# Sums of x in two SwiGLU heads tied behind the low parts of weights, and TensorE kept in the order in which the program is written

## The chip, the cores and the metric

The kernel runs on one core of one Trainium2 chip. The metric is the device time of one execution in microseconds; lower is better. The chip's records name five engines: PE (TensorE, the matmuls), PEld (its weight loads), DVE (VectorE), ACT (ScalarE), POOL (GpSimd) and SP (SyncE, which here only issues transfers).

## The reference, cut to what matters

A decoder trunk of two layers on 512 tokens of width 1024: a recurrent mixer, a SwiGLU, dilated attention with shared keys and values, and a second SwiGLU. The change touches the two SwiGLU stages alone:

```python
def swiglu(h, w_in, w_out):                 # w_in: 1024 x 5632, w_out: 2816 x 1024
    g, u = jnp.split(h @ w_in, 2, axis=-1)
    return (jax.nn.silu(g) * u) @ w_out
# in the trunk, for both layers
h = h + swiglu(rms_norm(h, ffn_norm), w_in, w_out)
```

## The kernel before, in words

**Two parts of each number.** Every matmul is done in a rounded format, so each operand is split into a high part (ScalarE rounds it: names that end in h, wh for weights) and a low part (VectorE subtracts the high part: names that end in l, wl). `mm3` issues three matmuls for each term: high by high, low by high, high by low. A weight piece is 128 x 1024; it becomes usable when ScalarE has made wh and VectorE wl.

**The first product of a SwiGLU.** The hidden width 2816 is 22 blocks of 128. Blocks 0 and 1 (two gate blocks, two up blocks) are plain: 24 matmuls of 128x512 each (`plain_block`), and `plain_pair` then forms silu(g) times u. From block 2 on, two gate and two up blocks make a pair q (1 to 10), and its product is worked out from seven products of half size instead of eight, as in Winograd's form of Strassen's scheme. The weights are the gate halves GA and GB, the up half UB, and sums of halves S1 to S4; S1 and S3 are made by transfers that add to what a first transfer has brought (the first issued by SP, the adding one by POOL), and VectorE makes S2 = S1 + GA and S4 = GB + S2 in place. The other factors are quarters of x (B11, B21, B22: four feature blocks by 256 tokens) and sums of quarters T1 to T4, which are made once for each SwiGLU, at its start: `make_t1` to `make_t4`, from the stream h with VectorE (differences, combinations, low parts) and ScalarE (gains, high parts). In the order, `gh<-h` and `gl<-gh,par` are such steps; T4 is written into a free quarter of xh and xl. Each of the seven products is 24 matmuls of 128x256.

**Accumulators.** GA.B11, S2.T2, S3.T3 and UB.T4 add up in one PSUM bank, S1.T1 and S4.B22 in a second, GB.B21 stands in a third. What the bank holds in between is needed too: after GA, after S2 and after S3 ScalarE copies the shared bank to SBUF (`COPY e<-ps`, L690), and after S3 VectorE adds to that copy what is in S1's bank (`e<-ps,e`, L692). So S2.T2 may not begin before the copy after GA, S3.T3 not before the copy after S2, UB.T4 not before the copy after S3, and S4.B22 not before the addition at L692. `gate` (L668 to L670) finishes half a gate block, `store` splits the finished pair for the second product (L277, L278).

**The second product** takes four hidden blocks at a time, as soon as they are stored: an out block ("O" in the table `PRODUCTS`) is two outputs of 12 matmuls of 128x512 each. The last six hidden blocks, which hold the last pair (ghx, glx), are multiplied after all pairs, in eight blocks of 18 matmuls (`p.last`).

**What sets the order.** The program is written as a list of steps (`p.steps`). A scheduler of the Tile layer places the instructions of all engines from it and may move instructions of one engine past each other where no data forbids it; what is written under `tc.high_priority()` is preferred. Each engine then works through its own queue in the order fixed at build time. `Stream` makes the splits of a weight piece one or two pieces ahead. The pool "wts" has three buffers for wh and wl, so the split of a piece waits until the piece three before it has been multiplied.

## Time and profile before

| | |
|---|---|
| median of 3 runs (lowest, highest) | 1196.01 us (1193.79, 1197.9) |
| the profiled execution's own time | 1193.76 us |
| its span, first to last instruction | 1191.5 us |
| PE busy | 1172.9 us, 98% |
| DVE busy | 862.8 us, 72% |
| ACT busy | 621.3 us, 52% |
| DMA, mean over the span | 142 GB/s |

Times inside the execution are given from the start of the span. The first SwiGLU starts near 152 us and its seven-product pairs at 176 us; they end at 471 us. The second one's pairs run from 861 us to 1155 us. "Busy" of PE is of modelled matmul ends, so that a matmul's duration is longer than the distance from its start to that of the next; the distance is what counts for PE's pace, and the same holds for the short overlap of DVE's and ACT's instructions.

### The profile page before, as it was taken

Reading aid. Unit: us, or ns where it says so; the run is one execution under the profiler, and the core shown is the slowest. Engines: PE = TensorE matmul, PEld = TensorE weight load, DVE = VectorE, ACT = ScalarE, POOL = GpSimd, SP = SyncE. Lnnn points to the kernel's source line nnn. Section 1 sums busy time; section 2 is a strip of 40 time slices with the busy share of each in tenths; the row PEclk is TensorE's granted clock in tenths of the full one; section 3 lists DMA queues with packets and bytes.
Section 4 is the critical chain, followed back from the end, with each engine's and each line's share of the span. In section 5 each row is a group of like instructions: output and inputs, shape, how many; then the busy total and the mean of one; then the engine's idle time right before and its main releaser. Section 6 shows DMA issues by size and latency. Waiting matters only on the chain.

```text
span 1191.5 us, 18092 instructions
## 1 busy us (share of the span) xinstructions
PE 1172.9 (98%) x7083; PEld 1040.8 (87%) x7083; DVE 862.8 (72%) x1505; ACT 621.3 (52%) x877; POOL 165.7 (14%) x181
## 2 busy tenths in 40 slices
PE   9999999999999999999999999999999999999998
PEld 6788888999999998888888888898899999999986
DVE  7987679777777776977565677765897777777763
ACT  6796545443444443565555667655563444444431
POOL 4210010000000000020411334341100000000000
PEclk9999999999999999999999999999999999999999
DMA  7643375565555542333988657535855555555413
GB/s 234 153 110 106 106 220 154 157 159 159 144 148 153 157 102 73 111 99 92 226 179 181 143 118 175 106 72 124 230 154 148 159 158 150 151 152 153 101 54 110
DMA packets 71574, 169.30 MB, mean 142 GB/s; under 512 B 6081, under 2 KB 6977, under 8 KB 71489
## 3 DMA queue, kind: packets, MB, share of 16 engines
q1 hardware_dynamic: 52752, 122.36, 32.4%
q0 software_dynamic: 17584, 44.57, 21.9%
q10 hardware_dynamic: 1152, 1.23, 0.3%
q8 instruction: 55, 0.90, 0.3%
q14 instruction: 31, 0.25, 0.1%
HBM read 164.99 MB, written 2.10 MB: 140 GB/s over the span
## 4 chain that ended last, share of the span: by engine, by line
PE 91%; DVE 4%; ACT 2%; DMA 1%; issue 1%; ACTq 0%; DVEq 0%
PE ps L156 25%; PE ps L157 25%; PE ps L158 25%; PE ps L949 5%; PE ps L950 5%; PE ps L951 5%; PE ps L1028 1%; DMA S<-in_f_in 1%; PE ps L1115 1%; DVE xc L444 1%; ACT wh L110 0%; ACT pr L1101 0%; DMA wr<-in_w_in 0%; PE ps L294 0%; DVE ql L278 0%
## 5 line engine op out<-in xcount | busy, mean ns | idle before, releaser
L156 PE MATMUL ps<-xh,wh 128*128 128x256 f32 (+1 forms) x896 | 283.5, 317 | 2.4 <-ACT xh L272 1.4
L158 PE MATMUL ps<-xh,wl 128*128 128x256 f32 (+1 forms) x896 | 281.3, 314 | 2.2 <-DVE wl L615 2.2
L157 PE MATMUL ps<-xl,wh 128*128 128x256 f32 (+1 forms) x896 | 281.3, 314 | 0.1
L110 ACT CAST wh<-wr 128x1024 fp32r<-128x1024 f32 (+2 forms) x132 | 130.8, 992 | 112.0 <-PE ps L157 73.7
L156 PEld LDWEIGHTS ps<-xh,wh 128*128 128x128 f32 x896 | 170.9, 191 | 16.7 <-ACT xh L272 2.3
L158 PEld LDWEIGHTS ps<-xh,wl 128*128 128x128 f32 x896 | 171.0, 191 | 12.4 <-DVE wl L615 2.4
L157 PEld LDWEIGHTS ps<-xl,wh 128*128 128x128 f32 x896 | 171.0, 191 | 10.8 <-DVE xl L278 0.4
L117 DVE TENSOR_TENSOR wl<-wr,wh 128x1024 fp32r<-128x1024 f32 (+3 forms) x89 | 100.1, 1126 | 40.7 <-ACT wh L110 40.2
L602 POOL DMA_DIRECT2D S<-in_f_in x40 | 47.8, 1194 | 583.4 <-DVE w L698 156.2
L156 PE MATMUL ps<-gh,wh 128*128 128x512 f32 x320 | 125.1, 391 | 1.7 <-ACT wh L110 1.7
L157 PE MATMUL ps<-gl,wh 128*128 128x512 f32 x320 | 125.0, 391 | 0.0
L158 PE MATMUL ps<-gh,wl 128*128 128x512 f32 x320 | 124.7, 390 | 0.0
L614 ACT CAST wh<-S 128x1024 fp32r<-128x1024 f32 x60 | 63.0, 1050 | 114.0 <-PE ps L157 69.7
L949 PE MATMUL ps<-wh,xh 128*128 128x512 f32 x224 | 91.5, 408 | 0.0
L951 PE MATMUL ps<-wh,xl 128*128 128x512 f32 x224 | 87.7, 391 | 0.0
L950 PE MATMUL ps<-wl,xh 128*128 128x512 f32 x224 | 87.4, 390 | 0.0
L614 ACT CAST wh<-GB 128x1024 fp32r<-128x1024 f32 x40 | 42.0, 1050 | 83.9 <-PE ps L157 78.2
L615 DVE TENSOR_TENSOR wl<-S,wh 128x1024 fp32r<-128x1024 f32 x60 | 73.3, 1222 | 16.6 <-ACT wh L614 16.6
L714 DVE TENSOR_TENSOR h<-h,ps 128x512 f32<-128x512 f32 x64 | 43.9, 685 | 45.0 <-PE ps L158 45.0
L156 PEld LDWEIGHTS ps<-gh,wh 128*128 128x128 f32 x320 | 60.2, 188 | 13.7 <-ACT wh L110 2.1
L158 PEld LDWEIGHTS ps<-gh,wl 128*128 128x128 f32 x320 | 60.1, 188 | 12.1
L157 PEld LDWEIGHTS ps<-gl,wh 128*128 128x128 f32 x320 | 60.2, 188 | 11.5
(286 smaller groups left out, 2689.9 us busy)
## 6 DMA issues: line engine op xcount, KB each, us to landing
S<-in_f_in SPq DMA_DIRECT2D x40, 512.0 KB, 3.6
S<-in_f_in POOLq DMA_DIRECT2D x40, 512.0 KB, 7.1
wr<-in_f_out SPq DMA_DIRECT2D x32, 512.0 KB, 4.2
wr<-in_w_q SPq DMA_DIRECT2D x28, 512.0 KB, 6.7
wl<-in_w_q POOLq DMA_DIRECT2D x28, 512.0 KB, 7.4
GA<-in_f_in SPq DMA_DIRECT2D x20, 512.0 KB, 3.7
GB<-in_f_in SPq DMA_DIRECT2D x20, 512.0 KB, 6.3
UB<-in_f_in SPq DMA_DIRECT2D x20, 512.0 KB, 5.0
```

Of the source, the lines that this page charges most:

```text
L110: nc.scalar.copy(hi[:, c], r[:, c])
L117: a = eng.tensor_tensor(lo[:, c], r[:, c], hi[:, c].bitcast(F32), ALU.subtract)
L156: PE.matmul(ps, wh, xh, start=first, stop=False, skip_group_check=on)
L157: PE.matmul(ps, wh, xl, start=False, stop=False, skip_group_check=on)
L158: PE.matmul(ps, wl, xh, start=False, stop=last, skip_group_check=on)
L602: nc.gpsimd.dma_start(r, p.half(1, q, n == "S1"), accum_op=ALU.add)
L614: S.copy(hi, r)
L615: V.tensor_tensor(lo, r, hi.bitcast(F32), ALU.subtract)
L714: V.tensor_tensor(h[m + b], h[m + b], ps, ALU.subtract)
L949: PE.matmul(ps[t], xh[k][:, r], wh[:, c], start=k == 0, stop=False)
L950: PE.matmul(ps[t], xh[k][:, r], wl[:, c], start=False, stop=False)
L951: PE.matmul(ps[t], xl[k][:, r], wh[:, c], start=False, stop=k == 7)
```

## The change: what it does

It has four parts.

1. **PE in program order.** The loop over `p.steps` and over `p.last` stands under `tc.manual_schedule` for PE: its instructions stand as they are written, while the other engines are still placed by the scheduler.
2. **Sums of x and plain pairs, held.** `Held` wraps VectorE and ScalarE. While a mark is set, every instruction issued through the wrapper is tied behind that mark in its own engine's order (`behind` makes an order and no wait). The marks are the low parts of the weight pieces of pair 1: `plain_pair(0)` goes behind the low part of S1, `make_t3` behind that of S2, `plain_pair(1)` behind that of GB, `make_t4` behind that of S3. `make_t1` and `make_t2` are not held. The table `early` places them after later steps than before. Held instructions show the line of the wrapper, L70, in the changed program.
3. **Another place for one out block**: in the last pair, the out block stands behind S3.T3 instead of GB.B21 (`LAST_PRODUCTS`).
4. **Banks**: the first plain block takes bank X, the other three take mm banks, instead of the rotation.

```diff
+LAST_PRODUCTS = ["S1.T1", "S2.T2", "GB.B21", "S3.T3", "O", "S4.B22", "UB.T4"]
 PRODUCTS = ["S1.T1", "S2.T2", "GB.B21", "O", "S3.T3", "GA.B11", "S4.B22", "O", "UB.T4"]
...
+class Held:
+    def __init__(self, tc, engine):
+        self.tc, self.engine, self.mark = tc, engine, None
+    def __getattr__(self, op):
+        fn, mark = getattr(self.engine, op), self.mark
+        def run(*a, **k):
+            inst = fn(*a, **k)
+            behind(self.tc, inst, mark)
+            return inst
+        return run if mark is not None else fn
...
-    V, S, G, PE = nc.vector, nc.scalar, nc.gpsimd, nc.tensor
+    V, S, G, PE = Held(tc, nc.vector), Held(tc, nc.scalar), nc.gpsimd, nc.tensor
+    def hold(mark, *fns):
+        V.mark = S.mark = mark
+        for fn in fns:
+            fn()
+        V.mark = S.mark = None
...
-                for name in PRODUCTS:
+                for name in PRODUCTS if q + 1 < HB // 2 else LAST_PRODUCTS:
...
-                    V.tensor_tensor(lo, r, hi.bitcast(F32), ALU.subtract)
+                    p.marks[q, n] = V.tensor_tensor(lo, r, hi.bitcast(F32), ALU.subtract)
...
-                ps = bank()
+                ps = bank("mm" if plain else "X")
...
-                if b == 1:
-                    plain["w"] = pair_tile()
-                    plain_pair(0)
-                elif b == HB + 1:
-                    plain_pair(1)
-                    store(0, plain["w"])
...
-            early = {0: [make_t1], 1: [make_t2], 2: [make_t3], 3: [make_t4]}
-            for s, (kind, *what) in enumerate(p.steps):
-                {"plain": plain_block, "product": product, "out": out_block}[kind](*what)
-                run(early.get(s, ()))
+            first = N_PLAIN
+            early = {0: [make_t1], 2: [make_t2],
+                     3: [lambda: hold(p.marks[first, "S1"], lambda: plain_pair(0))],
+                     5: [lambda: hold(p.marks[first, "S2"], make_t3)],
+                     6: [lambda: hold(p.marks[first, "GB"], lambda: plain_pair(1))],
+                     7: [lambda: hold(p.marks[first, "S3"], make_t4)]}
+            with tc.manual_schedule(engines={mybir.EngineType.PE}):
+                for s, (kind, *what) in enumerate(p.steps):
+                    {"plain": plain_block, "product": product, "out": out_block}[kind](*what)
+                    run(early.get(s, ()))
+                for m, i in enumerate(p.last):
...
```

In the quoted orders lines are those of each program's own file: the low part of a weight piece of the first product is L615 before and L639 after, the addition after S3 is L692 before and L714 after, and L70 is the wrapper.

**VectorE at the first SwiGLU's first pair.** Before, between the low part of GB for this pair and the addition after S3 (`e<-ps,e`, L692; S is the raw tile of S1 or S3 by its number):

```order
L615 TENSOR_TENSOR wl_1639<-GB,wh_1638 128x1024
L278 TENSOR_TENSOR gl<-w,gh 128x1024
L612 TENSOR_TENSOR GB<-GB,S_1383 128x1024
L615 TENSOR_TENSOR wl_1673<-S_1388,wh_1672 128x1024
L278 TENSOR_TENSOR xl<-gl,xh 128x4x256
L615 TENSOR_TENSOR wl_1705<-GA,wh_1704 128x1024
L668 TENSOR_TENSOR e<-ps,e 128x512
L669 TENSOR_TENSOR e<-e,rb 128x512
L615 TENSOR_TENSOR wl_1737<-GB,wh_1736 128x1024
L615 TENSOR_TENSOR wl_1769<-UB,wh_1768 128x1024
L692 TENSOR_TENSOR e<-ps,e 128x512
```

The sums of x are done by then; T4's low part (`xl<-gl,xh`) was the last of them, six rows ahead of the addition. Now, the last rows up to the same addition (L714) and T4's low part:

```order
L639 TENSOR_TENSOR wl_1739<-GB,wh_1738 128x1024
L70 TENSOR_TENSOR w<-w,g 128x512
L691 TENSOR_TENSOR e<-e,rb 128x512
L70 SCALAR_TENSOR_TENSOR gl<-gh,par 128x256 x2
L639 TENSOR_TENSOR wl_1771<-UB,wh_1770 128x1024
L70 TENSOR_TENSOR gl<-w,gh 128x1024
L70 SCALAR_TENSOR_TENSOR gl<-gh,par 128x256
L639 TENSOR_TENSOR wl_1802<-S_1642,wh_1801 128x1024
L70 SCALAR_TENSOR_TENSOR gl<-gh,par 128x256
L633 TENSOR_TENSOR S_1642<-S_1642,GA 128x1024
L714 TENSOR_TENSOR e<-ps,e 128x512
L70 TENSOR_TENSOR xl<-gl,xh 128x4x256
```

Moved: held steps (L70) and the next pair's S1 and S2 (S_1642) now stand ahead of the addition, and T4's low part behind it. The queue of the second SwiGLU reads the same.

**TensorE inside a later pair**, from the end of GA.B11 for the next pair to S4.B22. Before (xh, xl with 128x256 are the quarters B11 and B22; gh with 128x512 is the out block's first matmul):

```order
L157 MATMUL ps<-xl,wh_1972 128x256
L158 MATMUL ps<-xh,wl_1973 128x256
L156 MATMUL ps<-gh,wh_2036 128x512
L156 MATMUL ps<-xh,wh_2004 128x256
L157 MATMUL ps<-xl,wh_2004 128x256
```

Now:

```order
L180 MATMUL ps<-xl,wh_1974 128x256
L181 MATMUL ps<-xh,wl_1975 128x256
L179 MATMUL ps<-xh,wh_2006 128x256
L180 MATMUL ps<-xl,wh_2006 128x256
L181 MATMUL ps<-xh,wl_2007 128x256
```

The one matmul of the out block that stood between the two products is back at its block, behind S4.B22.

**TensorE where the last pair is first used** (ghx; glx is its low part). Before, the matmuls ahead of the first ghx are of the third of the last eight blocks (wh_4479), those of the first two blocks (wh_4407, wh_4442) standing before them:

```order
L158 MATMUL ps<-gh,wl_4443 128x512
L156 MATMUL ps<-gh,wh_4479 128x512
L157 MATMUL ps<-gl,wh_4479 128x512
L158 MATMUL ps<-gh,wl_4480 128x512
L156 MATMUL ps<-ghx,wh_4407 128x512
L156 MATMUL ps<-ghx,wh_4442 128x512
L156 MATMUL ps<-gh,wh_4479 128x512
```

Now, the first block alone:

```order
L179 MATMUL ps<-gh,wh_4409 128x512
L180 MATMUL ps<-gl,wh_4409 128x512
L181 MATMUL ps<-gh,wl_4410 128x512
L179 MATMUL ps<-ghx,wh_4409 128x512
L180 MATMUL ps<-glx,wh_4409 128x512
L181 MATMUL ps<-ghx,wl_4410 128x512
```

Before the first ghx stand 27 matmuls of the three blocks, partly ahead of the last pair's products; now the 12 of the first block, all behind UB.T4.

## The prediction

> **What bounds the kernel now.** I read the page first: where the span goes by engine, and which engine the chain of work that ended last runs through.

> ```profile
> span 1191.5 us, 18092 instructions
> PE 1172.9 (98%) x7083; PEld 1040.8 (87%) x7083; DVE 862.8 (72%) x1505; ACT 621.3 (52%) x877; POOL 165.7 (14%) x181
> ```

> PE is the bound, so only two things can move the time: PE's waits, and its pace. The change removes and adds no matmul. I therefore took PE's timeline in the two SwiGLU stages, where the instructions move, for its pace and its waits. Columns: start, duration, instruction, in brackets the idle time before it and its releaser.

> ```profile
> 176.05 0.28 PE L156 MATMUL ps<-xh,wh 128*128 128x256 f32 x1
> 176.16 0.28 PE L157 MATMUL ps<-xl,wh 128*128 128x256 f32 x1
> ...
> 184.97 0.38 PE L158 MATMUL ps<-xh,wl 128*128 128x256 f32 x1 [2.21 <-DVE wl L615]
> ...
> 196.41 0.59 PE L156 MATMUL ps<-xh,wh 128*128 128x256 f32 x2
> ```

> ```profile
> 867.83 0.38 PE L156 MATMUL ps<-T2h,wh 128*128 128x256 f32 x1 [1.02 <-ACT e L690]
> ...
> 880.02 0.39 PE L156 MATMUL ps<-xh,wh 128*128 128x256 f32 x1 [0.42 <-ACT e L690]
> 880.74 0.38 PE L156 MATMUL ps<-xh,wh 128*128 128x256 f32 x1 [0.34 <-DVE e L692]
> ```

> The seven-product pairs begin with GA.B11 at 176.05. A matmul of 128x256 follows the last one after 0.12 us, so a product of 24 lasts 2.88. The first head waits 2.21 us for the low part of a weight; the second has three shorter waits, together 1.8. The two rows of 880 and the one of 196.41 (two matmuls, one of UB.T4 and then S4.B22's first, at about 196.6) are the places where S4.B22 starts: after GA, S1, S2, GB, S3 and the next GA, in both kernels. They are my yardstick: whatever moved before them, the same six products and one more matmul (0.12 us) have been done.

> **The change part by part.**

> *The heads.* S4.B22 adds to the bank of S1.T1, so it waits until VectorE has read that bank for the sum after S3 (L692). VectorE works off its queue one by one, so I ask when it reaches that addition now. Its chain starts with the low part of S1, which no reordering can bring forward: the raw S1 comes by two transfers, and the cast waits for the second.

> ```profile
> 174.00 1.05 ACT L614 CAST wh<-S 128x1024 fp32r<-128x1024 f32 x1 [4.37 <-DMA S<-in_f_in]
> ```

> ```profile
> 858.78 1.05 ACT L614 CAST wh<-S 128x1024 fp32r<-128x1024 f32 x1 [4.62 <-DMA S<-in_f_in]
> ```

> VectorE's own rows, the start of the chain in each head, and a stretch of six that gives the step of every kind:

> ```profile
> 175.08 1.23 DVE L615 TENSOR_TENSOR wl<-S,wh 128x1024 fp32r<-128x1024 f32 x1 [3.54 <-ACT wh L614]
> ...
> 178.83 0.42 DVE L560 TENSOR_TENSOR gh<-h 128x256 f32<-128x256 f32 x1
> 179.17 0.68 DVE L659 TENSOR_TENSOR g<-ps,rb 128x512 f32<-128x512 f32 x1
> 179.77 0.68 DVE L661 SCALAR_TENSOR_TENSOR w<-ps,rb 128x512 f32<-128x512 f32 x1
> 180.37 0.47 DVE L568 SCALAR_TENSOR_TENSOR gl<-gh,par 128x256 f32<-128x256 f32 x1
> 180.77 1.23 DVE L615 TENSOR_TENSOR wl<-S,wh 128x1024 fp32r<-128x1024 f32 x1
> 181.91 0.68 DVE L662 TENSOR_TENSOR w<-w,g 128x512 f32<-128x512 f32 x1
> ```

> ```profile
> 859.86 1.22 DVE L615 TENSOR_TENSOR wl<-S,wh 128x1024 fp32r<-128x1024 f32 x1 [3.61 <-ACT wh L614]
> ```

> From start to start: 1.14 us for 1024 elements, 0.60 for 512, 0.40 for a combination of 256, 0.34 for a difference of 256. The changed queue has, from S1's low part up to the addition: 13 of 1024 (low parts of S1, S2, GB, S3, the next GA, S4, UB, the next S1; the sums S2, S4 and the next S2; T3's low part; the plain pair's store), 8 of 512 (six of the plain pairs and two of the gate), 8 combinations and 4 differences (T3 and T4). That is 13 x 1.14 + 8 x 0.60 + 8 x 0.40 + 4 x 0.34 = 24.2 us, and the addition itself 0.68. S4.B22 starts at 175.08 + 24.9 = 200.0 in the first head, at 859.86 + 24.9 = 884.8 in the second. Against about 196.6 and 880.74, with the one matmul added, that is 3.5 and 4.2 us late. Before, a part of this work stood ahead of S1's low part, in the 3.5 us in which VectorE waited for it, or ahead of that wait; the hold puts it behind.

> What else waits in the heads lies inside this. S2's and GB's low parts now come in time (at 180.4 and 183.5, needed at about 182 and 184.9), so the 2.21 us go. S3.T3 waits for the copy after S2, which stands on ScalarE behind two gains that wait for the last differences of T3; with the 18th row of the chain, 12.8 us after 175.08, these are done, the gains and the copy take one more:

> ```profile
> 166.79 0.90 ACT L564 ACTIVATE gh<-gh,par 128x256 f32<-128x256 f32 x2
> ```

> ```profile
> 184.76 0.58 ACT L690 COPY e<-ps 128x512 f32<-128x512 f32 x1
> ```

> With half of 0.90 and 0.58 the copy ends at 189.0; without waits S3.T3 would start at 176.05 + 4 x 2.88 = 187.6. So PE waits 1.4 us there, then does S3 and the next GA until 194.8, and waits 5.2 us for the addition. T4's low part follows the addition by 1.2 us and is covered by S4.B22's 2.88. The POOL and SP queues read as before, so transfers come as before. Sum of the heads: +7.7 us, from below 2 (if VectorE does 3 us of each chain in gaps that I count as full) to 9.

> *Inside later pairs.* Before, S4.B22 would come slightly too early for the same addition, and one out matmul fills the gap.

> ```profile
> 252.82 0.68 DVE L692 TENSOR_TENSOR e<-ps,e 128x512 f32<-128x512 f32 x1
> ```

> ```profile
> 253.23 0.28 PE L158 MATMUL ps<-xh,wl 128*128 128x256 f32 x1
> 253.35 0.39 PE L156 MATMUL ps<-gh,wh 128*128 128x512 f32 x1
> 253.58 0.36 PE L156 MATMUL ps<-xh,wh 128*128 128x256 f32 x1
> 253.78 0.28 PE L157 MATMUL ps<-xl,wh 128*128 128x256 f32 x1
> ```

> ```profile
> 222.37:253.51 31.14, 31.14 (x217) 29.14 (x216) 22.69 (x24) 13.12 (x16) 2.39 (x2) 1.00 0.57 153
> ```

> The addition ends at 253.50, GA's last product slot at 253.35. Without the filler S4.B22 waits about 0.2 us, and a first matmul after a wait takes 0.08 more than its step (253.58 to 253.78). A pair is 7 x 2.88 + 48 x 0.227 = 31.05 us of matmuls plus 0.2 to 0.28; before it is 31.14 (the row above, one pair). So +0.1 to +0.2 in each of 8 pairs of both stages: +2.2 us, from 0 to 4.5 (0.28 in 16 pairs, nothing given back).

> *The last pair and its out block.* Before, the out block stands after GB and PE waits 0.85 us for its weights, 1.0 from start to start; the tail is covered.

> ```profile
> 463.05 0.28 PE L158 MATMUL ps<-T3h,wl 128*128 128x256 f32 x1
> 464.18 0.50 PE L156 MATMUL ps<-gh,wh 128*128 128x512 f32 x1 [0.85 <-ACT wh L110]
> ```

> ```profile
> 471.27 0.68 DVE L701 TENSOR_TENSOR w<-ps,e 128x512 f32<-128x512 f32 x1
> 471.87 0.95 DVE L117 TENSOR_TENSOR wl<-wr,wh 128x768 fp32r<-128x768 f32 x1
> ...
> 473.45 1.22 DVE L702 TENSOR_TENSOR w<-w,rb 128x1024 f32<-128x1024 f32 x1
> ```

> ```profile
> 474.71 1.05 ACT L277 CAST ghx<-w 128x1024 fp32r<-128x1024 f32 x1 [2.70 <-DVE w L702]
> ```

> The out block's weights now have one product more (2.88 us), so the 1.0 goes. But the first ghx matmul stands 12 matmuls (2.7 us) behind UB.T4. From UB's last matmul: its 0.28, then VectorE's two multiplications (0.60 each), a low part of 768 (0.87), the factor (1.22) and ScalarE's 1.05, with some 0.15 of handing over: 4.8 us, against 0.12 + 2.7 of cover. PE waits 1.9 us for ghx, and 1.0 more for glx (1.23 less one matmul). That is 3.0 against 1.0 and 0.2 of interleaving: +1.8, and twice that, +3.6 us for both stages; from +1.8 (if the low part of 768 does not stand in the way) to +6 (if none of the 1.0 is given back).

> *The banks* cost nothing: GB takes bank X at 184.7, and the held plain pair reads the plain block out of it as the second step of VectorE's chain, at about 176.2; the rotation stood at the same place after its four steps.

> **Sum.** 7.7 + 2.2 + 3.6 = 13.5 us on the profiled execution's 1193.76, which is 1207.3; that execution lies 2.2 below the median of the runs, 1196.01, so for the median I forecast 1209.5 us.

> **Rivals.** *PE's clock falls in the 5.2 us gaps.* The start of the program shows a slow pace:

> ```profile
> 8.71 0.63 PE L157 MATMUL ps<-xl,wh 128*128 128x512 f32 x1
> 9.13 0.63 PE L158 MATMUL ps<-xh,wl 128*128 128x512 f32 x1
> ...
> 10.58 0.39 PE L157 MATMUL ps<-xl,wh 128*128 128x512 f32 x1
> 10.81 0.40 PE L158 MATMUL ps<-xh,wl 128*128 128x512 f32 x1
> ```

> There the step is 0.42 instead of 0.23 until about 10 us. If a gap of 5.2 us brought that pace back for some 3.3 us, it would cost 1.5 us in each head, 1212.5 in all. The longest wait of PE in the heads before is 2.21 us and the pace behind it is the usual one, so the trace shows no wait long enough. [...] Chance 0.22.

> *Faster: the waits of before go and none takes their place.* If VectorE reached the addition 5.2 us earlier, at S4's slot of 194.8, the heads would only give back 2.21, 1.02, 0.42 and 0.34 with their restarts, 4.5 us, and the last pairs' waits of 1.0 each: about 1189.5 on the median. It decides at a chain of 19.7 us instead of 24.9. What speaks for it: before, the same engine had the addition done at 196.6. Against it: the queue is fixed and its rows are counted. Chance 0.04.

> *No change*: the heads' lateness is only half of mine, and the later pairs and the tails cost nothing, +3 us, 1199. For it speaks that each of these is a difference of small times; against it, that all three point the same way. Chance 0.05. *The heads alone*: 1204, chance 0.12.

> **How the numbers follow.** The forecast as summed has the remaining 0.57. A difference under 0.3% (3.6 us) cannot be told from no change in this kernel. Faster 0.04, same 0.05, slower 0.91. The range goes from the heads alone to the clock's fall with a somewhat longer slow stretch: 1203.5 to 1214.5.

> **What would show it.** In the changed profile: before S4.B22 in both heads a wait of some 5 us for DVE L714, and before S3.T3 one of 1.4 us for the copy; no wait for a weight's low part; 0.1 to 0.2 us more in each pair; 1.9 and 1.0 us before ghx and glx. The prediction is wrong if the low part of S1 starts earlier than 175, if the rows after it run with steps other than those above, or if S4.B22 does not wait for L714.

## The result, and the profile after

The changed kernel takes 1214.72 us (median of 6 runs, 1211.24 to 1218.71), the kernel before beside it 1194.85 us (1192.2 to 1197.9): a ratio of 1.0166, 95% interval 1.0138 to 1.0193. It is 19.9 us slower. The prediction had the direction, and 1209.5 us, 13.5 more than the 1196.01 on which it stood; the measured time lies 0.2 us beyond the end of its range. So the question is where the other 6 us are.

The page of the profiled execution (1213.73 us), the span, the engines' busy time and, of the 40 slices, the one for the granted clock:

```profile
span 1211.5 us, 18091 instructions
...
PE 1180.6 (97%) x7083; PEld 1047.6 (86%) x7083; DVE 862.9 (71%) x1505; ACT 620.8 (51%) x877; POOL 164.3 (14%) x181
...
PEclk9999998999999999999999999999999999999999
```

TensorE has as many matmuls as before, but is busy for 1180.6 us instead of 1172.9: the same work has become slower, not only later. The 8 in the last row says where to look first, the seventh slice, 182 to 212 us, which is the first head (a head is the first pair of a SwiGLU's seven-product pairs; a tail, below, is its last pair and the last eight blocks).

Who waited for whom, TensorE alone (us in total, times, longest):

```profile
PE ps L179 <- DVE e L714: 10.0, 2, 5.0
PE ps L179 <- ACT ghx L301: 3.4, 2, 1.7
PE ps L179 <- ACT e L712: 2.2, 2, 1.3
...
PE ps L180 <- DVE glx L302: 1.5, 2, 0.8
```

These are the waits that the prediction named: the addition after S3 (L714) twice 5.0, the copy after S2 (L712; 1.34 in the first head, 0.84 in the second), ghx and glx. No wait for a weight's low part is left in the heads. TensorE's timeline at these places:

```profile
189.30 0.39 PE L179 MATMUL ps<-T3h,wh 128*128 128x256 f32 x1 [1.34 <-ACT e L712]
...
200.32 0.55 PE L179 MATMUL ps<-xh,wh 128*128 128x256 f32 x1 [5.00 <-DVE e L714]
...
202.38 0.42 PE L179 MATMUL ps<-xh,wh 128*128 128x256 f32 x1
202.59 0.42 PE L180 MATMUL ps<-xl,wh 128*128 128x256 f32 x1
...
206.40 0.28 PE L180 MATMUL ps<-xl,wh 128*128 128x256 f32 x1
206.52 0.28 PE L181 MATMUL ps<-xh,wl 128*128 128x256 f32 x1
...
481.71 0.49 PE L179 MATMUL ps<-ghx,wh 128*128 128x512 f32 x1 [1.72 <-ACT ghx L301]
482.97 0.80 PE L180 MATMUL ps<-glx,wh 128*128 128x512 f32 x1 [0.77 <-DVE glx L302]
...
895.64 0.38 PE L179 MATMUL ps<-xh,wh 128*128 128x256 f32 x1 [5.00 <-DVE e L714]
```

S4.B22 starts at 200.32 in the first head. Look at the steps behind it: 202.38 to 202.59 is 0.21 us for a matmul of 128x256, at 206.40 it is 0.12 again. TensorE runs at half its pace for some 6 us after the wait. The windows of the trace give the granted clock; their bounds are set here to the places where it changes (first column the window, then its length, then busy time of PE, PEld, DVE, ACT and POOL; PEclk comes third from the end):

```profile
196.11:199.52 3.41, 0.00 (x0) 0.00 (x0) 3.41 (x6) 1.77 (x3) 0.00 (x0) 1.00 0.55 178
199.52:202.93 3.41, 2.61 (x12) 2.64 (x13) 1.79 (x3) 0.00 (x0) 1.19 (x1) 0.50 0.56 162
202.93:206.35 3.42, 3.42 (x18) 3.42 (x17) 0.53 (x1) 0.70 (x1) 0.00 (x0) 0.50 0.83 139
...
479.41:482.83 3.42, 1.07 (x4) 0.34 (x2) 2.31 (x4) 1.04 (x1) 0.00 (x0) 1.00 0.77 237
482.83:486.24 3.41, 3.27 (x8) 2.61 (x9) 1.26 (x5) 0.84 (x2) 0.00 (x0) 0.50 0.01 1
...
892.43:895.84 3.41, 0.20 (x2) 0.23 (x2) 3.41 (x5) 1.05 (x1) 0.00 (x0) 1.00 0.39 139
895.84:899.25 3.41, 3.41 (x18) 3.41 (x18) 0.79 (x1) 0.00 (x0) 1.19 (x1) 0.50 0.68 187
```

The clock is 0.50 for 6.83 us in the first head, for 3.41 in the second, and for 3.41 in the first tail, where the waits were only 1.72 and 0.77. From the timeline, every start-to-start time less the step of its shape: the slow stretches cost 2.6 us (28 matmuls of 256 at 0.093 more), 1.4 (15 of them) and 1.5 in the tail. That is 5.5 us in this execution.

### The profile page after: what moved, and what is told of

Its sections match the earlier page's. It is cut to its first block, busy times and chain, and to the rows that moved or that the text cites. A ratio compares the mean times of both kernels' runs of the same rounds, so it can differ in the third digit from the quotient of the medians.

```text
span 1211.5 us, 18091 instructions
## 1 busy us (share of the span) xinstructions
PE 1180.6 (97%) x7083; PEld 1047.6 (86%) x7083; DVE 862.9 (71%) x1505; ACT 620.8 (51%) x877; POOL 164.3 (14%) x181
## 3 DMA queue, kind: packets, MB, share of 16 engines
q10 hardware_dynamic: 1152, 1.23, 0.4%
## 4 chain that ended last, share of the span: by engine, by line
PE 86%; DVE 7%; ACT 3%; DMA 2%; issue 1%; ACTq 0%; DVEq 0%
PE ps L179 23%; PE ps L180 23%; PE ps L181 23%; PE ps L977 5%; PE ps L978 5%; PE ps L979 5%; DMA GA<-in_f_in 2%; DVE wl L639 2%; PE ps L1056 1%; PE ps L1143 1%; DVE gl L70 1%; DVE xc L468 1%; ACT wh L638 1%; ACT pr L1129 0%; ACT wh L127 0%
## 5 line engine op out<-in xcount | busy, mean ns | idle before, releaser
L179 PE MATMUL ps<-xh,wh 128*128 128x256 f32 (+1 forms) x896 | 286.7, 320 | 12.4 <-DVE e L714 10.0
L639 DVE TENSOR_TENSOR wl<-S,wh 128x1024 fp32r<-128x1024 f32 x60 | 73.4, 1223 | 21.4 <-ACT wh L638 21.4
L181 PEld LDWEIGHTS ps<-gh,wl 128*128 128x128 f32 x320 | 60.3, 188 | 12.8
```

What stands on the lines that cost most here:

```text
L179: PE.matmul(ps, wh, xh, start=first, stop=False, skip_group_check=on)
L181: PE.matmul(ps, wl, xh, start=False, stop=last, skip_group_check=on)
L639: p.marks[q, n] = V.tensor_tensor(lo, r, hi.bitcast(F32), ALU.subtract)
```

## Experiments

The theory: the waits came out as summed, about 13.5 us, and the rest is TensorE's clock, which is halved behind them. Its main rival: the clock has nothing to do with it, and the slow steps come from what else is busy there, or the waits are longer than I counted. Other runs take the change apart; each has several executions, the one that measures the clock a single one. All were timed beside the kernel before, at 1194.3 to 1195.3 us in each series.

**Filling the waits.**

```diff
+            def filler(n, tag):
+                idle = bank(tag, "idle")
+                for _ in range(n):
+                    PE.matmul(idle, xh[4][:, 0:128], xh[4], start=True, stop=True)
...
+                if q == N_PLAIN and n in ("S3", "S4"):
+                    filler(5 if n == "S3" else 20, "O")
...
+                        if m == 0 and k == 4:
+                            filler(11, "S")
```

> The changed kernel, and TensorE does idle work in the waits: 5 dummy matmuls of 128x512 before S3.T3 and 20 before S4.B22 of each head, 11 before the first ghx of each tail, into a bank that nobody reads. No wait is shortened. Theory (the waits came out as summed, and what I missed is the granted clock, halved for 3.4 us or twice that behind the long waits): the clock stays full, the steps behind the waits are 0.12 and 0.227 again, S4.B22 still starts at about 200.3, and the time falls by 2.6 + 1.4 + 1.5 = 5.5 us, 1214.7 to about 1209. Rival (the slow steps come from something else that is busy at those places, VectorE's and the transfers' load): the steps stay 0.21 and the time stays within 1 us of 1214.7.

Measured: 1208.38 us, 1.0109 of before (1.0094 to 1.0124), 6.3 us less than the changed kernel. TensorE's timeline at S4.B22 of the first head, behind the dummies, and at glx in the first tail:

```profile
199.62 0.28 PE L179 MATMUL ps<-xh,wh 128*128 128x256 f32 x1
199.73 0.28 PE L180 MATMUL ps<-xl,wh 128*128 128x256 f32 x1
...
479.56 0.51 PE L180 MATMUL ps<-glx,wh 128*128 128x512 f32 x1 [0.25 <-DVE glx L302]
```

S4.B22 comes 0.7 us earlier than in the changed kernel, but so does everything in this execution (the first S1.T1 by 0.8): from S1.T1 to S4.B22 it is 21.23 us here and 21.15 there. It is no longer VectorE that S4.B22 waits for. In this program the addition stands two rows earlier in VectorE's queue (the next S1's low part and the next S2 come behind it):

```profile
197.11 0.68 DVE L721 TENSOR_TENSOR e<-ps,e 128x512 f32<-128x512 f32 x1
```

It is done 1.8 us before S4.B22 starts, so here the number of dummies sets the length of that stretch, and in the first head it comes out as the wait was. What differs is that TensorE works in it. The steps behind are 0.12 at once, and no slow stretch is left in heads and tails: 72 matmuls more make the kernel faster. Place by place the two profiled executions differ by 2.6 us in the first head, 0.8 in the second, where the dummies hold S4.B22 0.8 us longer than the wait did, and 1.5 in the first tail; the 6.3 us are between the medians. The rival of other load has little left, since VectorE has as many instructions (1505) and the transfers bring as much (169.3 MB); the next run settles it. And 1208.38 less 1195.2 is 13.2 us, close to the sum of the prediction (13.5) with the pace held full; to a part that is the choice of the dummies' number.

**Behind which waits the clock fell.** A measuring kernel, which has none of the long waits of the changed one, makes one wait in each of 16 pairs:

```diff
+            def gap(q, copies):
+                idle = bank("OS"[(q + 1) % 2], "idle")
+                PE.matmul(idle, xh[4][:, 0:128], xh[4], start=True, stop=True)
+                with tc.high_priority():
+                    S.copy(delay, idle[:, 0:128])
+                    for _ in range(copies):
+                        S.copy(delay, delay.bitcast(F32))
+                PE.matmul(idle, delay, xh[4], start=True, stop=True)
```

> A measuring kernel, its time is of no interest. Based on a version without the long waits (no holds, tail split, UB.T4 ahead of S4.B22), with one made wait in each of the pairs 2 to 9 of both SwiGLU stages, behind S2.T2: a dummy matmul, a chain of 1 + 0, 1, 2, 3, 4, 5, 7, 9 copies of 128x128 on ScalarE behind it, and a dummy matmul that waits for the last of them; waits from about 1.4 to 4 us. Theory (in the runs so far slow stretches begin on a grid of 3.413 us, and one follows a grid window in which TensorE was idle for more than about 0.6 of it, 2.05 us): waits below 1.9 us bring no slow stretch, waits of 2.1 to 3.5 bring one where enough of them falls into one window, and only waits above 4.1 us always do; each slow stretch is 3.41 us long. [...]

Measured, in one execution: waits of 1.48, 1.81, 2.14, 2.47, 2.80, 3.13, 3.79 and 4.45 us, each once in both stages. No slow stretch followed the two waits of 1.48 and the two of 2.14; one followed one of the two waits of 1.81, of 2.47 and of 2.80, and both waits of 3.13, of 3.79 and of 4.45. Nor does the slow pace begin where the wait ends. The timeline at three of these waits:

```profile
310.61 0.80 PE L704 MATMUL idle<-xh,delay 128*128 128x512 f32 x1 [2.47 <-ACT delay L703]
...
346.47 0.50 PE L704 MATMUL idle<-xh,delay 128*128 128x512 f32 x1 [2.80 <-ACT delay L703]
...
347.39 0.28 PE L182 MATMUL ps<-xh,wl 128*128 128x256 f32 x1
347.51 0.34 PE L180 MATMUL ps<-xh,wh 128*128 128x256 f32 x1
347.64 0.42 PE L181 MATMUL ps<-xl,wh 128*128 128x256 f32 x1
...
961.66 0.54 PE L704 MATMUL idle<-xh,delay 128*128 128x512 f32 x1 [1.81 <-ACT delay L703]
```

After the wait of 2.80 TensorE works at full pace from 346.47 to 347.5, and only then goes slow. The windows of 3.413 us, counted from the starts of the slow stretches:

```profile
272.50:275.92 3.42, 1.70 (x14) 1.38 (x12) 2.20 (x3) 1.96 (x4) 0.00 (x0) 1.00 0.51 165
275.92:279.33 3.41, 2.99 (x24) 2.94 (x25) 0.32 (x1) 0.34 (x2) 1.20 (x1) 1.00 0.87 261
306.63:310.05 3.42, 1.51 (x12) 1.19 (x10) 2.20 (x2) 2.12 (x5) 0.00 (x0) 1.00 0.53 180
310.05:313.46 3.41, 2.85 (x12) 2.76 (x13) 0.12 (x1) 0.47 (x2) 1.20 (x1) 0.50 0.86 270
344.18:347.59 3.41, 1.12 (x8) 1.08 (x9) 1.23 (x1) 2.11 (x7) 1.20 (x1) 1.00 0.79 267
347.59:351.00 3.41, 3.41 (x18) 3.41 (x17) 0.00 (x0) 0.00 (x0) 0.00 (x0) 0.50 0.66 158
...
958.58:961.99 3.41, 1.60 (x11) 1.25 (x10) 2.08 (x2) 1.99 (x4) 0.00 (x0) 1.00 0.58 187
961.99:965.40 3.41, 3.41 (x17) 3.40 (x16) 0.00 (x0) 0.00 (x0) 1.20 (x1) 0.50 0.87 258
```

A window in which TensorE is busy 1.51, 1.12 or 1.60 of its 3.41 us is followed by one at half the clock; one with 1.70, where the wait was 2.14, is not. In the slow window from 347.59 VectorE, ScalarE and GpSimd do nothing (0.00), so here the slow pace came without load on any of the three, and the main rival falls.

I set such windows over the eleven profiled executions of this study, from the fourth window on (ahead of it, in the kernel before, the rows give a clock of 1.00 though matmuls of 128x512 take 0.42 us instead of 0.23) and without the silence behind the last matmul. Of 28 windows at full clock that were followed by a halved one, 26 had TensorE busy for 0 to 1.68 us; the other two, with 2.15 and 2.17, lie in the attention, among transposes and matmuls of 64 columns, and stay unexplained. The least busy ones that were not followed had 1.57, 1.62 and 1.64. So from 1.57 to 1.68 us, near half of 3.41, both were seen; every window with less was followed, and of those with more only the two of the attention. A slow window with TensorE busy 1.52 to 2.61 us was followed by a second slow one (10 cases); with 2.85 us or more it was not.

The theory holds in kind but not in its bounds: it had no slow stretch below 1.9 us of wait, and one of 1.81 brought one; it had each stretch last 3.41 us, and behind one wait of 3.13 and both of 3.79 it lasted 6.83. The length of the wait alone did not decide: the same wait of 2.80 was followed in one stage and not in the other.

In the changed kernel's execution the slow stretches begin at 199.52, 482.83 and 895.84; the distances, 283.31 and 413.01 us, are 83 and 121 times 3.413. In the measuring kernel a single wait of 1.81 us was enough where it fell into one window (958.58 to 961.99). What sets the clock is not shown by these traces.

**The holds taken off.** The sums and the plain pairs are issued with the plain blocks again; TensorE's program order and the moved out blocks stay.

```diff
-            early = {0: [make_t1], 2: [make_t2],
-                     3: [lambda: hold(p.marks[first, "S1"], lambda: plain_pair(0))],
-                     5: [lambda: hold(p.marks[first, "S2"], make_t3)],
-                     6: [lambda: hold(p.marks[first, "GB"], lambda: plain_pair(1))],
-                     7: [lambda: hold(p.marks[first, "S3"], make_t4)]}
+            early = {0: [make_t1], 1: [make_t2], 2: [lambda: plain_pair(0), make_t3],
+                     3: [lambda: plain_pair(1), make_t4]}
```

> The changed kernel without the holds: the sums of x and the plain pairs are issued with the plain blocks again, as before the change; TensorE's program order and the moved out blocks stay. Theory (the head's loss is VectorE's queue behind the low part of S1): the wait before S4.B22 falls from 5.0 to about 1.6 us, one of 1.3 us before S2.T2 takes the place of that before S3.T3, no slow stretch in the heads; 3.4 + 2.6 us less in the first head, 3.4 + 1.4 in the second, the time falls by about 10.8 to 1204. Rival (TensorE's fixed order makes the head slow, whatever VectorE does): the wait before S4.B22 stays near 5 us, the time within 2 us of 1214.7.

Measured: 1201.99 us, 1.0056 (1.0043 to 1.0068). TensorE's waits in the heads:

```profile
PE ps L179 <- ACT e L712: 3.2, 2, 1.9
PE ps L179 <- DVE e L714: 2.3, 2, 1.2
```

The wait for the addition falls from 5.0 to 1.2 (1.6 expected), those before S2.T2 are 1.3 and 1.9, and 12.7 us go, 1.9 more than expected. The head's loss was VectorE's queue behind S1's low part, as the prediction counted it, and not the fixed order alone. Both tails wait as in the changed kernel (3.4 us in all for ghx, 1.5 for glx), and in one of them, here the second, the clock fell (0.50 from 1163.57 on, for 3.41 us).

**The holds alone.** The kernel before with the holds, TensorE's order left to the scheduler.

```diff
-            with tc.manual_schedule(engines={mybir.EngineType.PE}):
-                for s, (kind, *what) in enumerate(p.steps):
+            for s, (kind, *what) in enumerate(p.steps):
...
-                for name in PRODUCTS if q + 1 < HB // 2 else LAST_PRODUCTS:
+                for name in PRODUCTS:
```

> The kernel before with the holds alone (sums and plain pairs at their new steps, tied behind the low parts, the plain block's bank as after); TensorE's order is the scheduler's again, the out blocks stand where they stood before. The scheduler answers the late addition by setting the next pair's S1.T1 ahead of S4.B22. Theory (the holds make VectorE's queue late, and TensorE's fixed order only decides how much of that becomes idle time): in each head 1.3 us before S3.T3 and, around S1.T1, two waits of 1.3 and 1.6 instead of one of 5.0; per head about 4.6 us less what before lost there (2.2 to 2.5), no idle grid window, so +4 to +6 for both heads, 1199 to 1201, and the tail as before. Rival (the holds cost all of the head's 5 us whatever TensorE's order is): 1204 or more. Second rival (the fixed order is what costs): within 1 us of 1195.2.

Measured: 1198.59 us (12 runs), 1.0027 (1.0016 to 1.0039), 3.3 us more than before, a little under the expected 4 to 6, and outside both rivals. TensorE's waits in the heads:

```profile
PE ps L179 <- ACT e L712: 3.3, 2, 1.7
PE ps L181 <- DVE wl L639: 2.4, 2, 1.2
PE ps L179 <- ACT wh L638: 2.2, 2, 1.1
```

No wait of 5 us: the scheduler sets S1.T1 of the next pair into the gap, and in this profiled execution the clock never fell (1.000; the twelve had 0.995 to 1.0). So the parts do not add. The holds alone cost 3.3 us, the order and the moved blocks alone 6.8 (1201.99 less 1195.2), all together 19.9: the fixed order turns the late addition into idle time, 5.0 us in each head, and behind it the clock fell to 0.50 in the changed kernel's execution.

**The out block ahead of S4.B22.**

```diff
-PRODUCTS = ["S1.T1", "S2.T2", "GB.B21", "O", "S3.T3", "GA.B11", "S4.B22", "O", "UB.T4"]
+PRODUCTS = ["S1.T1", "S2.T2", "GB.B21", "O", "S3.T3", "GA.B11", "O", "S4.B22", "UB.T4"]
```

> The changed kernel with the second out block of a pair ahead of S4.B22 instead of behind it. Theory (S4.B22 comes 0.2 us too early for the addition in each of the 16 later pairs, and 24 matmuls between would cover it): a pair takes 31.05 to 31.1 us, 16 times 0.2 less, about 3 us: 1211.5. Rival (the out block only moves the wait to another product of the pair, or the 0.2 us is not a wait): no change, 1214 to 1215.5.

Measured: 1210.02 us, 1.012 (1.0105 to 1.0134), 4.7 less than the changed kernel. One pair, from S1.T1 to the next S1.T1, in the changed kernel and with the block moved:

```profile
240.16:271.53 31.37, 31.32 (x218) 29.20 (x217) 22.70 (x24) 13.12 (x15) 2.39 (x2) 1.00 0.59 152
```

```profile
240.11:271.19 31.08, 31.08 (x218) 29.16 (x217) 22.45 (x25) 13.14 (x15) 2.39 (x2) 1.00 0.59 154
```

The pair is 0.29 us shorter, 4.1 us over the 14 such pairs of both stages (the expectation counted 16); the wait was there, and 0.2 was a little low. What makes up the remaining 0.6 us is not shown: in this execution the heads were 1.3 and 2.8 us longer than in the changed kernel's, since the clock fell behind the waits for the copy too (1.75 and 1.95 us; 0.50 for 3.41 us each), and the tails kept the full clock.

**The last pair's block put back.** The list for the last pair is left out, holds and order stay.

```diff
-                for name in PRODUCTS if q + 1 < HB // 2 else LAST_PRODUCTS:
+                for name in PRODUCTS:
```

> The changed kernel with the last pair's out block at its place of before, behind GB instead of S3; holds and program order stay. Theory (in the last pair no product of a next one stands between S3.T3 and S4.B22, so without the out block there S4.B22 waits for the copy after S3 and the addition behind it): a wait of about 2.6 us before S4.B22 in both last pairs and perhaps the 1.0 us for the out block's weights again, +5 to +7 us, and now and then a slow stretch: 1220 to 1223. Rival (the place of that block is worth nothing, the wait for its weights comes back and another one goes): 1213 to 1217.

Measured: 1223.49 us, 1.0239 (1.0223 to 1.0255), 8.8 more than the changed kernel and slightly over the expected end. The timeline at S4.B22 of the last pair:

```profile
474.59 0.39 PE L179 MATMUL ps<-xh,wh 128*128 128x256 f32 x1 [2.44 <-DVE e L714]
```

From the last pair's S1.T1 to the last matmul with ghx it is 62.8 us in both stages, against 58.56 in the changed kernel's second stage, where the clock stayed full. Of these 4.3 us a slow stretch of the tail is 1.5. So with the fixed order the other place of that block is worth some 2.8 us in each stage, and more where the clock falls; the wait for its weights did not come back. Under that order, this part of the change pays.

**The tail split.** The two first blocks' parts without ghx ahead of the first ghx.

```diff
+                ws.asp = 1
+                part(0, range(4))
+                part(1, range(4))
+                for m in range(8):
+                    part(m, range(4 if m < 2 else 0, 6))
+                    after(m, opened[m][0])
+                    ws.asp = 2
```

> The changed kernel, and in the tail the parts of blocks 0 and 1 that need no ghx (12 matmuls each) both come ahead of block 0's ghx part. Theory: the 1.7 + 0.8 us and 1.9 + 1.0 us of waits for ghx and glx fall to about 0.2 a tail, and with them the slow stretch of the first tail: 2.4 + 2.6 + 1.5 = about 6 us less, 1208.5 to 1210. Rival (the weights of block 1 come too late, or the end of the tail only waits instead): 0 to 2 us less.

Measured: 1207.11 us, 1.0102 (1.0085 to 1.012), 7.6 less than the changed kernel, more than the expected 6. No wait for ghx or glx is left, and the same stretch of the tail takes 55.8 us in both stages, where the changed kernel has 60.07 and 58.56. The heads' longest wait is still there:

```profile
PE ps L179 <- DVE e L714: 9.6, 2, 5.0
```

**All of it mended.** TensorE in program order, no holds, tail split, the out block behind S4.B22 and UB.T4 ahead of it, priority for the copies and the addition, and the last two steps of a pair's product moved behind S4.B22; the second run has the sums ahead of the plain pairs besides. Of the edit, the first line is against the changed kernel, the other four are the second run against the first.

```diff
+PRODUCTS = ["S1.T1", "S2.T2", "GB.B21", "O", "S3.T3", "GA.B11", "UB.T4", "S4.B22", "O"]
...
-            early = {0: [make_t1], 1: [make_t2], 2: [lambda: plain_pair(0), make_t3],
-                     3: [lambda: plain_pair(1), make_t4]}
+            early = {0: [make_t1], 1: [make_t2], 2: [make_t3, lambda: plain_pair(0)],
+                     3: [make_t4, lambda: plain_pair(1)]}
```

> TensorE in program order, no holds, tail split as in the run of that name, out block behind S4.B22 and UB.T4 ahead of it (with the last two steps of the pair's product moved to S4, except in the last pair), and the copies after GA, S2 and S3 and the addition given priority. Theory (with each wait named so far covered, only one of about 1.4 us before S2.T2 is left in a head, 0.3 to 0.4 in a tail, and the later pairs go at 31.05 us): against no_hold, 1202.0, the pairs give 4.7 (as measured for the out block's place), the tails about 5, the addition 1.3 in each head: 1202.0 - 4.7 - 5 - 2.6 = 1189.7, faster than the kernel before by 5.5 us. Rival (TensorE in program order loses the scheduler's fillings somewhere else, or UB.T4 first delays the next pair): 1193 to 1196, no gain on before.

> The run best7 with the sums of x issued ahead of the plain pairs (T3 before plain pair 0, T4 before plain pair 1). Theory (S2.T2 waits for the copy after GA, which stands on ScalarE behind the gains of T3 that wait for VectorE; with the sums ahead of the plain pairs the gains are done sooner): the wait of 1.3 and 1.9 us before S2.T2 goes, short ones for low parts of together about 1.1 us come in the first head: 1 to 3 us less than best7, 1186 to 1188. Rival (the plain pairs' sixteen steps of VectorE then come ahead of the low parts and the wait only moves): 1188.5 to 1191.

Measured: 1188.99 us, 0.9946 of before (0.9929 to 0.9964), and 1186.35 us, 0.9929 (0.9916 to 0.9941). The only wait of the heads in the first and those in the second:

```profile
PE ps L179 <- ACT e L713: 2.9, 2, 1.7
```

```profile
PE ps L181 <- DVE wl L639: 0.9, 2, 0.6
PE ps L179 <- ACT e L713: 0.2, 1, 0.2
```

Both came as expected. The first is 6.3 us faster than the kernel before in its series, the second 7.9 in its own. So this kernel with a fixed order of TensorE can be faster than the one before with the scheduler's, once VectorE's work is early and each wait has cover. That the fixed order itself gains is not shown: the split tail, the early sums and the other places of the products were not run under the scheduler's order.

## Why the prediction was wrong

*VectorE's chain in the heads*: right. It was to take 24.9 us from S1's low part to the end of the addition. VectorE's timeline, its start and its end in each head of the changed kernel:

```profile
175.22 1.23 DVE L639 TENSOR_TENSOR wl<-S,wh 128x1024 fp32r<-128x1024 f32 x1 [7.31 <-ACT wh L638]
...
199.48 0.69 DVE L714 TENSOR_TENSOR e<-ps,e 128x512 f32<-128x512 f32 x1
...
870.54 1.23 DVE L639 TENSOR_TENSOR wl<-S,wh 128x1024 fp32r<-128x1024 f32 x1 [5.90 <-ACT wh L638]
...
894.82 0.68 DVE L714 TENSOR_TENSOR e<-ps,e 128x512 f32<-128x512 f32 x1
```

That is 24.95 and 24.96 us, and S4.B22 starts 25.1 us behind the first row in both heads. Without the slow steps, the heads lost 3.6 and 3.9 us against before; summed were 3.5 and 4.2. The wait for the copy was 1.34 in the first head, 1.4 predicted, but 0.84 in the second, where S1.T1 starts 4.45 us behind the chain's first row instead of 3.95.

*Later pairs*: mechanism right, size low. A pair takes 31.37 us against 31.14, 0.23 more where 0.1 to 0.2 was counted. Only 14 of the 16 pairs are of this kind, the two others lose 0.11 each: 3.4 us instead of 2.2.

*The tails*: right. From start to start the waits are 1.88 and 1.03 (1.9 and 1.0 predicted). Without the slow stretch the tails lost 1.9 and 1.7 us net; predicted were 1.8 each.

*The banks* were not run alone; the heads of the changed kernel wait only for L712 and L714, so no wait there names them.

*The step that failed* is the rival on the clock, which I took out of the sum. The argument was that before, a wait of 2.21 us had left the pace as it was, so that "the trace shows no wait long enough" and only the two waits of 5.2 us were priced, at a chance of 0.22. One wait that left no mark shows little: in the measuring kernel waits of 1.81, 2.47 and 2.80 us were followed by a slow stretch in one stage and not in the other. That wait, 182.76 to 184.97, lay across two windows of 3.413 us of the kernel before (counted from the place near 9.7 us where the slow pace of its start ends):

```profile
180.38:183.80 3.42, 2.09 (x16) 1.68 (x14) 3.42 (x8) 2.87 (x4) 0.00 (x0) 1.00 0.36 132
183.80:187.21 3.41, 2.24 (x18) 2.23 (x19) 3.41 (x4) 2.48 (x3) 0.00 (x0) 1.00 0.00 0
```

TensorE is busy 2.09 and 2.24 us in them, above the 1.57 to 1.68 of the count in both; that the pace held was, by that count, luck of where the wait lay. A wait of 5.0 us, wherever the windows lie, leaves at least 2.5 of some window's 3.41 us idle and TensorE busy for 0.91 at most, so by that count the fall was to come in both heads; the tails' 1.7 + 0.8 us made it possible there, and in one of two it came. It cost 5.5 us in the profiled execution and 6.3 between the medians (changed kernel less the filled one), where the rival had 3: it counted no tail, and one slow stretch of 3.3 us in each head, a length that none of its rows shows, where the first head had 6.83 and the second 3.41.

Place by place, the spans of the two profiled executions differ by 20.0 us, and that is: heads 7.5 (predicted 7.7), later pairs 3.4 (2.2), tails 3.6 (3.6), the slow clock 5.5 (nothing).

*The range* ended at that rival with little added, for the same reason.

## What to carry to other kernels

## What was not expected of the hardware

The same waits were followed by a slow stretch in one place and not in another (2.80 us in the measuring kernel, 1.72 and 0.77 in the tails of the changed one), and the clock differs from execution to execution: the six of the changed kernel had mean granted clocks of 0.989 to 0.995; the two with 0.995 had the shortest spans, 1209.0 and 1209.6 us, the others 1211.5 to 1216.5. The kernel before shows it too: in one series its spans went from 1191.3 us at 0.999 to 1194.5 at 0.997. In the last version, whose waits in the heads are 0.6 us at most, five of five executions had 1.0 and spans from 1183.1 to 1185.5. So the spread between runs is probably in part the place of the waits in such windows, an estimate from these clocks and spans; no run here separates it from other causes.
